# A silu in the context FFN of a two-layer diffusion backbone: formed from tanh in place of exp, add and reciprocal

## The chip, the core and the metric

One NeuronCore of a Trainium2 chip runs the whole program: TensorE (PE), VectorE (DVE), ScalarE (ACT), GpSimd (POOL), and SyncE (SP), whose queue issues most of the DMAs. The metric is the device time of one execution in microseconds (us), as the median of several runs; lower is better.

## The reference, cut to what matters

Two layers work on 1024 latent tokens of width 1024 and on 256 context tokens. Each layer has a mixer (layer 0: gated convolution beside differential attention; layer 1: pooling beside retention) and a gated ConvFFN with 2816 inner features. Context tokens go through layer 0 with the same weights, read only context tokens, and have an FFN of their own there.

```python
def conv_ffn(h, w_up, conv_w, conv_b, w_down):
    a, b = jnp.split(h @ w_up, 2, axis=-1)
    a = dwconv3(a, conv_w) + conv_b
    return (jax.nn.silu(a) * b) @ w_down
...
        x = x + g1 * y_lat
        x = x + g2 * conv_ffn(modulate(rms_norm(x, norm2_g[i]), sh2, sc2), ...)
        if not last:
            ctx = ctx + g1c * y_ctx
            ctx = ctx + g2c * conv_ffn(modulate(rms_norm(ctx, norm2_g[i]), sh2c, sc2c), ...)
```

silu(a) is a / (1 + exp(-a)), which is also a/2 times (1 + tanh(a/2)).

## The kernel before, in words

Everything is float32. A product on TensorE is made of three matmuls on split operands (`mm3`, lines 223 to 225): each operand is held as a rounded high part and the remainder, and high x high, high x low and low x high are added up. Weights stream in through SP's queue and are split on the way (`WStream.split`): line 111 rounds on ScalarE (`wh`), line 113 forms the remainder (`wl`) on VectorE, or on GpSimd for every second weight while `on_pool` is 2.

The work around the change is `attention`. Two generators are woven into each other by a fixed ratio: `att_lat`, the differential attention of the latent tokens (8 blocks of 4 query tiles; `AttBlock.scores`, `combine`, `product`), and `chain`, which takes the context tokens through output projection, norm and FFN (`ffn`, 22 feature tiles of 128). The attention's VectorE work is a maximum over the scores (tile `S`, line 1509), the combination of two softmaxes (line 1524) and the remainder of the transposed probabilities (line 1543); its exponentials are on ScalarE (line 1511).

In `ffn`, `up(f)` multiplies a tile of 128 features of both halves (tile `pab`, 48 matmuls of 256 columns), copies the halves out of PSUM on ScalarE (line 729 `a`, line 731 `b`), convolves (`conv_silu`: line 708 on ScalarE, lines 709 and 710 on VectorE, into the tile `fcv`, called `t` in the code), and forms silu(t) * b: line 736 exp(-t) on ScalarE into `e`, line 737 adds one on ScalarE, line 738 forms t * b on GpSimd, line 739 the reciprocal on VectorE, line 740 the last product on VectorE. Lines 742 and 743 split the result on ScalarE and GpSimd. After four feature tiles `down` (tile `pd`, line 757 on VectorE) multiplies them with the down weights and adds to the context. Silu itself is used as a function (line 712) only in the FFNs of the latent tokens, later in the program.

The order in which each engine gets its instructions is not written by hand: the tile framework's scheduler lays out the instructions of all engines from dependencies, program order and its own costs, and each engine then works through its queue in that order, waiting in place where an input is late. So an edit of a few instructions can change the order of others.

Of the kernel before, what the change touches and what calls it, by code (L numbers as in the profile page):

```python
# [11 lines left out]
AF = mybir.ActivationFunctionType  # L12
ALU = mybir.AluOpType
# [123 lines left out]
class Net:  # L137
# [576 lines left out]
    def ffn(self, L, xk, N, hs, G, alloc, big, ps, gate):  # L714

        nc = self.nc
        g = {}

        def up(f):
            W = self.ws.get()  # L720
            a = big.tile([P, N + 2], F32, tag="a", name="a")
            nc.gpsimd.memset(a[:, 0:1], 0.0)
            nc.gpsimd.memset(a[:, N + 1:N + 2], 0.0)

            pt = ps.tile([P, 512], F32, tag="mm", name="pab")
            self.gemm(pt[:, :N], W, hs, N, 4)
            W = self.ws.get()
            self.gemm(pt[:, N:2 * N], W, hs, N)
            nc.scalar.copy(a[:, 1:N + 1], pt[:, :N])
            b = big.tile([P, N], F32, tag="b", name="b")  # L730
            nc.scalar.copy(b, pt[:, N:2 * N])
            t = big.tile([P, N], F32, tag="cv", name="fcv")
            self.conv_silu(L, f, a, t, N, False)

            e = big.tile([P, N], F32, tag="e", name="e")
            nc.scalar.activation(e, t, AF.Exp, scale=-1.0)
            nc.scalar.activation(e, e, AF.Identity, bias=self.ones)
            nc.gpsimd.tensor_tensor(t, t, b, op=ALU.mult)
            nc.vector.reciprocal(e, e)
            nc.vector.tensor_tensor(t, t, e, op=ALU.mult)  # L740
            gt = g[f] = alloc()
            nc.scalar.copy(gt[:, 0, :], t)
            nc.gpsimd.tensor_tensor(gt[:, 1, :], t, gt.bitcast(F32)[:, 0, :], op=ALU.subtract)

        def down(f0, n):
            W = [self.ws.get() for _ in range(n)]
            for m0 in range(0, 8, 2):
                pt = ps.tile([P, 512], F32, tag="mm", name="pd")
                for m in (m0, m0 + 1):
                    po = pt[:, (m - m0) * N:(m - m0 + 1) * N]  # L750
                    ms = slice(m * P, (m + 1) * P)
                    for j in range(n):
                        gt = g[f0 + j]
                        self.mm3(po, (W[j][0][:, ms], W[j][1][:, ms]), (gt[:, 0, :], gt[:, 1, :]), j == 0, j == n - 1)
                for m in (m0, m0 + 1):
                    po = pt[:, (m - m0) * N:(m - m0 + 1) * N]
                    nc.vector.scalar_tensor_tensor(xk(m), in0=po, scalar=gate(m), in1=xk(m), op0=ALU.mult, op1=ALU.add)
                yield

        for kind, f, n in self.ffn_plan(G):  # L760
            if kind == "u":
                up(f)
                yield
            else:
                yield from down(f, n)
# [923 lines left out]
```

## Time and profile before

| what | value |
|---|---|
| median of 3 runs | 2772.87 us (2769.24 to 2776.75) |
| the profiled execution, its own time | 2781.38 us |
| its span from the first to the last instruction | 2779.6 us |
| TensorE busy | 2625.0 us, 94% |
| VectorE busy | 1910.8 us, 69% |
| ScalarE busy | 1098.5 us, 40% |
| GpSimd busy | 800.5 us, 29% |
| granted TensorE clock, mean | 0.966 of full speed |

The busy time of TensorE is the time in which at least one matmul was under way; matmuls overlap each other in the pipeline, so this share is an upper bound on how much of the engine is used. The shares are means over stages of different kinds. The stage that the change touches is the weave of attention and context FFN; its feature tiles run from about 490 to 890 us.

### The profile page before, as it was taken

Reading aid. Unit: us, or ns where it says so; the run is one execution under the profiler, and the core shown is the slowest. Engines: PE = TensorE matmul, PEld = TensorE weight load, DVE = VectorE, ACT = ScalarE, POOL = GpSimd, SP = SyncE. Lnnn points to the kernel's source line nnn. Section 1 sums busy time; section 2 is a strip of 40 time slices with the busy share of each in tenths; the row PEclk is TensorE's granted clock in tenths of the full one; section 3 lists DMA queues with packets and bytes.
Section 4 is the critical chain, followed back from the end, with each engine's and each line's share of the span. In section 5 each row is a group of like instructions: output and inputs, shape, how many; then the busy total and the mean of one; then the engine's idle time right before and its main releaser. Section 6 shows DMA issues by size and latency. Waiting matters only on the chain. (4 is left out here: it accounts for less than half of the span.)

```text
span 2779.6 us, 35344 instructions
## 1 busy us (share of the span) xinstructions
PE 2625.0 (94%) x12924; PEld 2206.8 (79%) x12924; DVE 1910.8 (69%) x2815; ACT 1098.5 (40%) x1635; POOL 800.5 (29%) x674
## 2 busy tenths in 40 slices
PE   7999998999898999999998989999999999999999
PEld 6877787888888787787886767787778888888887
DVE  7467856999887577777776665613356767766895
ACT  5322224666665344333333323323234333334342
POOL 3221113444342034444440000102212555544000
PEclk7999998999998999999999999999999999999999
DMA  6224625443322723333338774337363222224874
GB/s 246 93 93 144 197 96 164 127 131 109 109 89 79 245 84 121 114 124 121 123 105 272 246 224 153 121 112 223 115 235 114 76 84 90 85 91 152 286 231 165
DMA packets 203007, 402.26 MB, mean 145 GB/s; under 512 B 19536, under 2 KB 88784, under 8 KB 202448
## 3 DMA queue, kind: packets, MB, share of 16 engines
q1 hardware_dynamic: 199952, 394.87, 43.2%
q10 hardware_dynamic: 2880, 5.12, 0.6%
q8 instruction: 102, 1.67, 0.3%
q14 instruction: 73, 0.60, 0.1%
HBM read 330.19 MB, written 69.73 MB: 144 GB/s over the span
## 5 line engine op out<-in xcount | busy, mean ns | idle before, releaser
L225 PE MATMUL P<-s,wl 128*128 128x512 f32 x1120 | 440.4, 393 | 10.5 <-DVE wl L113 10.2
L223 PE MATMUL P<-s,wh 128*128 128x512 f32 x1120 | 438.9, 392 | 7.8 <-ACT p L884 4.5
L224 PE MATMUL P<-s,wh 128*128 128x512 f32 x1120 | 438.4, 391 | 0.0
L111 ACT CAST wh<-wr 128x1024 fp32r<-128x1024 f32 (+1 forms) x268 | 278.4, 1040 | 392.7 <-DMA wr<-in_w_dn 83.8
L113 DVE TENSOR_TENSOR wl<-wr,wh 128x1024 fp32r<-128x1024 f32 (+1 forms) x231 | 289.3, 1255 | 183.8 <-ACT wh L111 176.3
L223 PE MATMUL pd<-s,wh 128*128 128x512 f32 x660 | 263.2, 399 | 24.9 <-DVE x L938 16.3
L225 PE MATMUL pd<-s,wl 128*128 128x512 f32 x660 | 261.8, 397 | 2.5 <-DVE wl L113 2.5
L224 PE MATMUL pd<-s,wh 128*128 128x512 f32 x660 | 262.2, 397 | 0.6 <-DVE s L927 0.6
L225 PEld LDWEIGHTS P<-s,wl 128*128 128x128 f32 x1120 | 211.8, 189 | 59.2 <-DVE wl L113 15.5
L223 PEld LDWEIGHTS P<-s,wh 128*128 128x128 f32 x1120 | 212.1, 189 | 53.9 <-ACT p L884 5.4
L224 PEld LDWEIGHTS P<-s,wh 128*128 128x128 f32 x1120 | 211.9, 189 | 44.6
L363 POOL TENSOR_TENSOR rr<-vv,mhalf 128x8 f32<-128x8 f32 (+2 forms) x39 | 56.6, 1451 | 520.1 <-DVE vv L361 520.1
L223 PEld LDWEIGHTS pd<-s,wh 128*128 128x128 f32 x660 | 127.1, 193 | 54.3 <-DVE x L938 17.6
L225 PEld LDWEIGHTS pd<-s,wl 128*128 128x128 f32 x660 | 126.8, 192 | 30.7 <-DVE wl L113 4.1
L224 PEld LDWEIGHTS pd<-s,wh 128*128 128x128 f32 x660 | 127.1, 193 | 28.4 <-DVE s L927 1.5
L113 POOL TENSOR_TENSOR wl<-s,wh 128x1024 fp32r<-128x1024 f32 x40 | 101.6, 2540 | 148.0 <-ACT wh L111 148.0
L709 DVE SCALAR_TENSOR_TENSOR fcv<-a,vec,fcv 128x1024 f32<-128x1024 f32 (+1 forms) x66 | 71.1, 1078 | 102.6 <-ACT fcv L708 102.6
L111 ACT CAST wh<-r 128x1024 fp32r<-128x1024 f32 x80 | 67.1, 839 | 178.7 <-DVE r L784 99.7
L708 ACT ACTIVATE fcv<-a,vec 128x1024 f32<-128x1024 f32 (+1 forms) x66 | 68.5, 1037 | 174.5 <-POOL a L899 166.4
L113 POOL TENSOR_TENSOR wl<-wr,wh 128x1024 fp32r<-128x1024 f32 x37 | 94.3, 2550 | 134.0 <-ACT wh L111 125.5
L1511 ACT ACTIVATE p<-S,s 128x1280 f32<-128x1280 f32 (+1 forms) x80 | 92.6, 1158 | 69.5 <-DVE s L1509 65.4
L783 POOL TENSOR_TENSOR r<-r 128x512 f32<-128x512 f32 x40 | 72.5, 1813 | 132.1 <-DMA r<-in_w_up 100.9
(373 smaller groups left out, 6680.2 us busy)
## 6 DMA issues: line engine op xcount, KB each, us to landing
wr<-in_w_dn SPq DMA_DIRECT2D x101, 512.0 KB, 4.5
wr<-in_w_up SPq DMA_DIRECT2D x98, 512.0 KB, 3.6
gr<-gD SPq DMA_DIRECT2D x121, 256.0 KB, 4.0
gD<-fcv SPq DMA_DIRECT2D x44, 512.0 KB, 2.8
wr<-in_w_out SPq DMA_DIRECT2D x40, 512.0 KB, 3.7
r<-in_w_up SPq DMA_DIRECT2D x40, 512.0 KB, 3.3
s<-in_mod1T SPq DMA_DIRECT2D x136, 128.0 KB, 3.5
mbw<-in_mod0T SPq DMA_DIRECT2D x32, 512.0 KB, 3.9
```

The lines of the kernel that those rows point to most:

```text
L111: self.nc.scalar.copy(hi, raw)
L113: eng.tensor_tensor(lo, raw, hi.bitcast(F32), op=ALU.subtract)
L223: mm(out, L[0], R[0], start=first, stop=False)
L224: mm(out, L[0], R[1], start=False, stop=False)
L225: self.last_mm = mm(out, L[1], R[0], start=False, stop=last)
L363: self.last_pow = nc.gpsimd.tensor_tensor(r, vv, self.mhalf[:, :n], op=ALU.pow)
L708: nc.scalar.activation(t, a[:, 1:N + 1], AF.Identity, bias=self.v(f"fcb{L}", f), scale=w[1])
L709: nc.vector.scalar_tensor_tensor(t, in0=a[:, 0:N], scalar=w[0], in1=t, op0=ALU.mult, op1=ALU.add)
L783: nc.gpsimd.tensor_tensor(r1[:, 1536:], r1[:, 512:1024], r1[:, :512], op=ALU.add)
L1511: nc.scalar.activation(e, sv, AF.Exp, bias=s2[:, m:m + 1], accum_out=self.s1[:, qt:qt + 1] if m == 0 else s2[:, 2:3])
```

## The change

Line 731 halves `b` as it copies it; the exp becomes tanh(t/2); the ScalarE addition (line 737 before) and the reciprocal are gone, and the last product becomes one VectorE instruction that adds one to the tanh and multiplies. `t` times half of `b`, times one plus tanh(t/2), is the same product. All later lines move up by two.

```diff
             nc.scalar.copy(a[:, 1:N + 1], pt[:, :N])
             b = big.tile([P, N], F32, tag="b", name="b")
-            nc.scalar.copy(b, pt[:, N:2 * N])
+            nc.scalar.mul(b, pt[:, N:2 * N], 0.5)
             t = big.tile([P, N], F32, tag="cv", name="fcv")
             self.conv_silu(L, f, a, t, N, False)
 
             e = big.tile([P, N], F32, tag="e", name="e")
-            nc.scalar.activation(e, t, AF.Exp, scale=-1.0)
-            nc.scalar.activation(e, e, AF.Identity, bias=self.ones)
+            nc.scalar.activation(e, t, AF.Tanh, scale=0.5)
             nc.gpsimd.tensor_tensor(t, t, b, op=ALU.mult)
-            nc.vector.reciprocal(e, e)
-            nc.vector.tensor_tensor(t, t, e, op=ALU.mult)
+            nc.vector.scalar_tensor_tensor(t, in0=e, scalar=1.0, in1=t, op0=ALU.add, op1=ALU.mult)
             gt = g[f] = alloc()
```

The scheduler lays the stage out anew. Two places show how.

**VectorE, ninth feature tile.** The names: `s` and `S` belong to the attention's maximum, `xc<-pd` to the context FFN's down step, `fcv` is `t`. Before:

```order
L709 SCALAR_TENSOR_TENSOR fcv<-a,vec,fcv 128x256
L1509 TENSOR_REDUCE s_5456<-S 128x1
L710 SCALAR_TENSOR_TENSOR fcv<-a,vec,fcv 128x256
L1562 SCALAR_TENSOR_TENSOR e_5482<-ost,e_5482 128x4
L757 SCALAR_TENSOR_TENSOR xc<-pd,modB,xc 128x256 x3
L739 RECIPROCAL e<-e 128x256
L1509 TENSOR_REDUCE s_5456<-S 128x1
L740 TENSOR_TENSOR fcv<-fcv,e 128x256
```

and in the changed kernel (line 738 is the new product, 1507 the maximum, 755 the down step):

```order
L1507 TENSOR_REDUCE s_5438<-S 128x1
L709 SCALAR_TENSOR_TENSOR fcv<-a,vec,fcv 128x256
L1560 SCALAR_TENSOR_TENSOR e_5464<-ost,e_5464 128x4
L710 SCALAR_TENSOR_TENSOR fcv<-a,vec,fcv 128x256
L755 SCALAR_TENSOR_TENSOR xc<-pd,modB,xc 128x256 x2
L738 SCALAR_TENSOR_TENSOR fcv<-e,fcv 128x256
L1507 TENSOR_REDUCE s_5438<-S 128x1
```

Between the end of the convolution (line 710) and the last product stood a small instruction, three down steps, the reciprocal and a maximum; now two down steps stand there.

**ScalarE, tenth feature tile.** `p<-S` is the attention's exponential, `pth` its rounded transposed probabilities. Before:

```order
L729 COPY a<-pab 128x256
L731 COPY b<-pab 128x256
L708 ACTIVATE fcv<-a,vec 128x256
L1511 ACTIVATE p_5708,s_5689<-S,s_5689 128x1280
L736 ACTIVATE e<-fcv 128x256
L111 CAST wh<-wr 128x1024
L737 ACTIVATE e<-e,ones 128x256
L1542 CAST pth<-tpp 128x4x128 x2
```

and in the changed kernel:

```order
L729 COPY a<-pab 128x256
L731 ACTIVATE b<-pab 128x256
L708 ACTIVATE fcv<-a,vec 128x256
L111 CAST wh<-wr 128x1024 x2
L1540 CAST pth<-tpp 128x4x128 x2
L1509 ACTIVATE p_5779,s_5668<-S,s_5770 128x1280
L1540 CAST pth<-tpp 128x2x128
L736 ACTIVATE e<-fcv 128x256
L1509 ACTIVATE p_5789,s_5770<-S,s_5770 128x1280
L740 CAST s4c<-fcv 128x256
```

The tanh stands later among the attention's instructions than the exp did, the addition is gone, and no table load stands between the tanh and the exponentials on either side of it.

## Rows read from the trace of the kernel before

**Rows 1.** Busy time by stretch: us, then each engine, granted clock, DMA share, GB/s.

```profile
core 0: us, PE busy (x) PEld busy (x) DVE busy (x) ACT busy (x) POOL busy (x), PEclk, DMA share, GB/s
490.00:890.00 400.00, 362.06 (x2648) 341.62 (x2647) 356.76 (x434) 248.47 (x433) 162.66 (x137) 0.96 0.35 110
```

**Rows 2.** Instruction groups of VectorE, 490 to 890 us: count, busy us, mean ns, idle before.

```profile
L1509 DVE TENSOR_REDUCE s<-S 128x1 f32<-128x1280 f32 x59 | 87.1, 1477 | 7.2 <-PE S L1508 7.2
L739 DVE RECIPROCAL e<-e 128x256 f32<-128x256 f32 x22 | 38.4, 1746 | 1.8 <-ACT e L737 1.7
L757 DVE SCALAR_TENSOR_TENSOR xc<-pd,modB,xc 128x256 f32<-128x256 f32 x40 | 17.9, 475 | 1.2 <-PE pd L225 1.2
L710 DVE SCALAR_TENSOR_TENSOR fcv<-a,vec,fcv 128x256 f32<-128x256 f32 x22 | 17.6, 802 | 0.1
L740 DVE TENSOR_TENSOR fcv<-fcv,e 128x256 f32<-128x256 f32 x22 | 16.6, 756 | 0.2
L709 DVE SCALAR_TENSOR_TENSOR fcv<-a,vec,fcv 128x256 f32<-128x256 f32 x22 | 14.6, 665 | 8.0 <-ACT fcv L708 8.0
```

**Rows 3.** Instruction groups of TensorE in the same stretch.

```profile
L223 PE MATMUL pab<-s4c,wh 128*128 128x256 f32 x325 | 95.9, 295 | 0.0
L1507 PE MATMUL S<-k,qa 128*128 128x512 f32 x118 | 52.0, 441 | 14.0 <-ACT p L1511 13.7
L1541 PE MATMUL tpp<-ident,p 128*128 128x128 f32 x296 | 49.5, 295 | 21.7 <-DVE ptl L1543 12.8 <-DVE p L1524 7.4 <-DVE osb L1570 0.8
L379 PE MATMUL orb<-ident,r 128*128 128x128 f32 x56 | 7.7, 274 | 0.0
```

**Rows 4.** Timeline of TensorE: start, us, engine, line and operation.

```profile
655.09 0.28 PE L225 MATMUL pab<-s4c,wl 128*128 128x256 f32 x1
655.21 0.28 PE L223 MATMUL pab<-s4c,wh 128*128 128x256 f32 x1
```

**Rows 5.** Waits of ScalarE for VectorE, 490 to 890 us: total us, times, longest.

```profile
ACT p L1511 <- DVE s L1509: 39.2, 24, 4.1
```

**Rows 6.** Instruction groups of ScalarE, 490 to 890 us.

```profile
L737 ACT ACTIVATE e<-e,ones 128x256 f32<-128x256 f32 x22 | 11.2, 510 | 0.2
L736 ACT ACTIVATE e<-fcv 128x256 f32<-128x256 f32 x22 | 9.1, 415 | 10.0 <-DVE fcv L710 9.9
L731 ACT COPY b<-pab 128x256 f32<-128x256 f32 x21 | 8.0, 383 | 2.2 <-POOL fcv L738 2.2
L1552 ACT ACTIVATE osb<-pv,subg 128x256 f32<-128x256 f32 x14 | 6.6, 469 | 0.0
```

**Rows 7.** Instruction groups of GpSimd, 490 to 890 us.

```profile
L113 POOL TENSOR_TENSOR wl<-wr,wh 128x1024 fp32r<-128x1024 f32 x31 | 79.7, 2570 | 108.7 <-ACT wh L111 100.2 <-PE pd L225 8.2
L738 POOL TENSOR_TENSOR fcv<-fcv,b 128x256 f32<-128x256 f32 x22 | 22.9, 1042 | 25.3 <-ACT e L736 25.0 <-DMA wr<-in_w_up 0.3
```

**Rows 8.** Timelines of ScalarE and GpSimd at the ninth feature tile.

```profile
608.34 0.41 ACT L736 ACTIVATE e<-fcv 128x256 f32<-128x256 f32 x1
609.28 2.95 POOL L682 TENSOR_TENSOR vl<-vraw,vh 128x1280 fp32r<-128x1280 f32 x1
612.18 0.74 POOL L738 TENSOR_TENSOR fcv<-fcv,b 128x256 f32<-128x256 f32 x1
```

**Rows 9.** Timelines of VectorE, ScalarE and GpSimd at the tenth feature tile.

```profile
651.55 1.70 DVE L740 TENSOR_TENSOR fcv<-fcv,e 128x256 f32<-128x256 f32 x1
642.03 0.42 ACT L736 ACTIVATE e<-fcv 128x256 f32<-128x256 f32 x1 [2.27 <-DVE fcv L710]
642.59 1.90 POOL L738 TENSOR_TENSOR fcv<-fcv,b 128x256 f32<-128x256 f32 x1 [0.32 <-ACT e L736]
650.58 2.40 POOL L113 TENSOR_TENSOR wl<-wr,wh 128x1024 fp32r<-128x1024 f32 x1 [6.08 <-ACT wh L111]
```

**Rows 10.** One line each: durations in ns, least, median, most.

```profile
L739 DVE RECIPROCAL e<-e x22: 1736/1744/1755, 492.4 to 883.4; 128x256 f32<-128x256 f32 x22
L740 DVE TENSOR_TENSOR fcv<-fcv,e x22: 403/418/2420, 495.7 to 887.5; 128x256 f32<-128x256 f32 x22
```

## The prediction

> **What bounds the stage now.** I read the busy time by stretch first, then the groups of the busiest engine, then who waits for whom. The weave of attention and context FFN lasts some 400 us of the 2780, and in it VectorE is busy for 357 us and idle for 43 [rows 1]. TensorE shows 362 us, but that is a union of overlapping spans: a 256-column matmul is listed with 0.28 us while the next one starts 0.12 us later [rows 4]. Counting starts instead of spans: of the stage's 2648 matmuls [rows 1], 236 have 512 columns (two lines of 118) and 408 are small ones (296 transposes, and two lines of 56) [rows 3]; the other 2004 have 256 columns. Taking 0.12 us for those, twice that for 512 columns and 0.1 us for the small ones (an estimate from the spacing, at full clock) gives 240 + 57 + 41 = 338 us. So VectorE at 89% and TensorE at about 85% share the stage, ScalarE has 248 us and GpSimd 163 [rows 1]. The waits say that VectorE is more often the late one: ScalarE's exponentials stood 39.2 us for the maximum on VectorE [rows 5], TensorE's score matmuls then waited 13.7 us for these exponentials, and its transposes 12.8 and 7.4 us for VectorE directly [rows 3]. VectorE's own waits are short and spread over many releasers [rows 2]. A microsecond taken off VectorE here is therefore worth something at the end, and not a full one.
>
> **The change, part by part.** (1) The reciprocal goes: 22 times 1.746 us, 38.4 us of VectorE [rows 2]. That is nearly 11% of what it does in the stage. It is a plain saving on that queue, since nothing else in the row takes its place.
>
> (2) The last product changes from a two-input product (0.756 us mean) to an add-and-multiply of the same shape. Lines 709 and 710 are that form, with 0.665 and 0.802 us [rows 2]. Their mean, 0.734, makes 22 times -0.02, so -0.5 us, with ends of -2.0 and +1.0. I take 0.
>
> (3) ScalarE loses the addition, 22 times 0.510 = 11.2 us. The halving copy costs between nothing (0.383 us, as the copy) and 0.086 us more (0.469, the scaled copy out of PSUM of line 1552), at most 1.9 us in all [rows 6]. The tanh is taken at the exp's 0.415 us. ScalarE is idle for 152 of the 400 us, so I count nothing for its own time; if that cover were gone, it would be another 9 to 11 us. The one thing on a path is that 0.51 us leave the chain from convolution to product.
>
> (4) A wait appears. Before, the product on VectorE stood behind the reciprocal, which covered GpSimd's product t * b; line 740 waited 0.2 us in all [rows 2]. Now nothing but the scheduler's filling stands between line 710 and the new product, which needs both the tanh and, behind it, GpSimd's product (GpSimd overwrites t, which the tanh reads, so it starts after it: 642.59 behind an exp that ended at 642.45 [rows 9]). With GpSimd free, the need is 0.415 + 0.14 + 1.042 [rows 6, 7], plus a hand-over of some 0.1: 1.7 us after the convolution. What the new order puts into the gap I priced by the means of the same forms: it lies between 0 and 3.2 us, 1.8 us on average, and is below 1.7 in 12 of the 22 tiles (the ninth has two down steps there, 2 times 0.475 [rows 2]). The shortfall of these twelve adds up to 8.5 us in which VectorE stands. The ends: 0, if tanh and product run while the convolution's neighbours do, and 18 us, if GpSimd is found as late in each tile as in this trace. I take 8.5. Whatever stands behind the product in VectorE's queue waits with it: the next maximum, and so the next exponential.
>
> (5) The order of the stage is made anew, and so is that of the output projection behind it. Nothing in the rows gives a sign to this. I take 0, with 5 us on either side.
>
> So VectorE has 38.4 - 8.5 = 30 us less to go through. How much of it reaches the end? Between 0 and all. After the change VectorE needs 357 - 38 + 8.5 = 327 us, TensorE still 338: neither is slack enough to hide the other, and TensorE can go no lower. Taking about half, since the two come out level, gives **-16 us**. What is late next is TensorE's own train of matmuls, and the weight splits on ScalarE and GpSimd. Against the profiled execution that makes 2781.4 - 16 = 2765; that execution was 8.5 us above the median of the runs, so the forecast for the median is 2772.9 - 16 = **2757 us**.
>
> **A rule weighed against the rows.** A reciprocal has one input, and its 22 durations lie between 1736 and 1755 ns, whatever GpSimd was doing; the two-input product had 418 ns as its median and 2420 at most [rows 10]. At 651.55 it took 1.70 us while GpSimd's weight split ran from 650.58 to 652.98 [rows 9]. So the reciprocals are VectorE time in which GpSimd gets through its work unhindered, and that time is what goes. The Trainium skill (SBUF — State Buffer, section SBUF: two separate sides) says why the two differ: a GpSimd instruction and a VectorE instruction with two SBUF inputs take an exclusive lock on a shared port pair, and the later one fully waits. The trace agrees for the product. This gives the second rival.
>
> **The rivals.**
> - *All of it reaches the end.* If VectorE alone sets the pace, the 30 us pass through, or 38 where the new wait is covered too: 2743 to 2734 us. For it: ScalarE waits 39.2 us for the maximum [rows 5]. Against it: TensorE's 338 us. Chance 0.18.
> - *The port eats it, or TensorE paces.* GpSimd is busy for 163 of 400 us [rows 1], 41%; the reciprocals covered some 0.41 times 38.4 = 16 us of its work, which now meets two-input instructions. VectorE's net saving falls to 30 - 16 = 14 us, half of it 7: 2766 us. If TensorE's train is the pace by itself, 2773. These are one case for the chances, no difference that can be told: 0.23.
> - *The product waits for GpSimd, and VectorE's queue with it.* In the ninth tile the exp ended at 608.75, GpSimd then went into a 2.95 us split that stood first in its queue, and t * b started at 612.18, 3.4 us after it [rows 8]. If the new order put t * b behind a weight split of 2.57 us [rows 7] in every tile, the product would be ready 0.42 + 2.57 + 1.04 = 4.0 us after the convolution; less 1.8 us of filling, VectorE would stand 2.2 us in each, 22 times 2.2 = 49 us against the 38 saved: +11 us, 2784 us. It decides from 38.4 / 22 = 1.75 us of wait in a tile. Against it: GpSimd had 25.3 us of idle time before t * b, nearly all of it waiting for the exp [rows 7], so mostly it is there first. Chance 0.09.
> - *The change brings table loads.* Alternating functions could make ScalarE load a table each time. The built order shows no load in this stage, in either kernel, so nothing is put on it.
>
> **How the numbers follow.** A measurement of this kernel can tell about 0.3%, 8.3 us, from no change. The forecast's case (8 to 30 us less) has 0.50; with the first rival's 0.18 faster has 0.68. Same has 0.23, slower 0.09. The likeliest is 2757 us. The range reaches from the whole reciprocal gained (2734, less 1 for the other terms) to just above no change: 2733 to 2776. It leaves out the slower rival and a better new order.
>
> **What would show it.** In the profile of the changed kernel, VectorE's busy time in the stage should fall from 357 to about 318 us, and the stage itself from 400 to about 384. The new product should show 0.65 to 0.85 us and an idle time before it of some 5 to 12 us in total, with GpSimd's t * b as the releaser. ScalarE's wait for the maximum should shrink below 39 us. The first rival would show a stage of 370 us or less; the second, the same stage with longer two-input instructions on VectorE; the third, more than 38 us of idle time before the new product. The forecast is wrong in its mechanism if the stage shrinks though VectorE's busy share does not fall, or if the time comes from anywhere outside 490 to 930 us.

## The result, and the profile after

The changed kernel takes **2789.71 us** (median; 2779.22 to 2791.55), the kernel before 2772.87 us. The ratio is 1.0055, with a 95% interval from 1.0034 to 1.0077: slower by about 15 us, where 16 us less were forecast. One caution for what follows: the profiled execution of the change was its fastest (2779.22 us), that of the kernel before was slower than any of its timed ones (2781.38 us), so the two profiles show nearly the same span and understate the difference.

Busy time by stretch, changed kernel, the columns as in [rows 1]:

```profile
490.00:890.00 400.00, 357.60 (x2656) 335.98 (x2655) 327.31 (x413) 237.09 (x408) 154.50 (x133) 0.98 0.33 103
```

VectorE is busy for 29.5 us less than in [rows 1]. The stage itself, from the context FFN's first convolution to the last attention block, lasted 429 us before (488 to 917 us) and 434 us now (484 to 918 us): what left VectorE's work came back as idle time, and a little more.

Instruction groups of VectorE in the same stretch (the maximum is now line 1507, the down step 755, the new product 738):

```profile
L1507 DVE TENSOR_REDUCE s<-S 128x1 f32<-128x1280 f32 x59 | 87.6, 1485 | 14.5 <-PE S L1506 14.1
L709 DVE SCALAR_TENSOR_TENSOR fcv<-a,vec,fcv 128x256 f32<-128x256 f32 x21 | 23.9, 1137 | 2.5 <-ACT fcv L708 2.5
L755 DVE SCALAR_TENSOR_TENSOR xc<-pd,modB,xc 128x256 f32<-128x256 f32 x42 | 18.7, 475 | 1.3 <-PE pd L225 1.2
L710 DVE SCALAR_TENSOR_TENSOR fcv<-a,vec,fcv 128x256 f32<-128x256 f32 x21 | 17.0, 810 | 0.1
L738 DVE SCALAR_TENSOR_TENSOR fcv<-e,fcv 128x256 f32<-128x256 f32 x21 | 14.9, 710 | 10.1 <-POOL fcv L737 10.0
```

Against [rows 2]: the reciprocal and its 38.4 us are gone; the new product costs 0.710 us and stands for GpSimd for 10 us, near the forecast 8.5; the maximum waits twice as long for TensorE's scores (14.1 for 7.2). And line 709, which the change does not touch, went from 0.665 to 1.137 us. Its durations in ns (least, median, most), before and then changed:

```profile
L709 DVE SCALAR_TENSOR_TENSOR fcv<-a,vec,fcv x22: 380/482/1879, 489.1 to 875.4; 128x256 f32<-128x256 f32 x22
```

```profile
L709 DVE SCALAR_TENSOR_TENSOR fcv<-a,vec,fcv x22: 472/670/3149, 484.7 to 877.8; 128x256 f32<-128x256 f32 x22
```

Timelines of VectorE and of GpSimd in the changed kernel, ninth feature tile:

```profile
604.19 2.32 DVE L709 SCALAR_TENSOR_TENSOR fcv<-a,vec,fcv 128x256 f32<-128x256 f32 x1
...
608.71 0.42 DVE L738 SCALAR_TENSOR_TENSOR fcv<-e,fcv 128x256 f32<-128x256 f32 x1 [0.90 <-POOL fcv L737]
```

```profile
603.82 2.40 POOL L113 TENSOR_TENSOR wl<-wr,wh 128x1024 fp32r<-128x1024 f32 x1
...
607.94 0.74 POOL L737 TENSOR_TENSOR fcv<-fcv,b 128x256 f32<-128x256 f32 x1
```

This piece of the convolution starts 0.37 us behind a weight split on GpSimd and ends 0.29 us behind its end (606.51 against 606.22), for work that took 0.48 us at the median before. The rule that the prediction weighed (the Trainium skill, SBUF — State Buffer, section SBUF: two separate sides: the later of the two waits for the shared ports until the other instruction is done) says this, and the trace agrees to within some 0.2 us. Of line 709's 22 instructions 4 took over 0.9 us before, and 10 do now, each beside a split on GpSimd: the new order makes them meet GpSimd's work more often.

Waits in the same stretch, two lines of the kernel before that [rows 2] do not hold, and then those of the changed kernel (total us, times, longest):

```profile
DVE s L1520 <- ACT p L1511: 7.0, 9, 1.5
DVE ptl L1543 <- ACT pth L1542: 4.1, 7, 1.5
```

```profile
DVE s L1518 <- ACT p L1509: 15.8, 16, 3.0
DVE s L1507 <- PE S L1506: 14.1, 10, 2.4
DVE fcv L738 <- POOL fcv L737: 10.0, 13, 2.1
DVE ptl L1541 <- ACT pth L1540: 9.4, 10, 1.6
DVE osb L1568 <- PE orb L379: 6.2, 1, 6.2
PE tpp L1539 <- DVE ptl L1541: 20.8, 17, 2.3
PE S L1505 <- ACT p L1509: 8.8, 5, 4.5
ACT p L1509 <- DVE s L1507: 43.8, 32, 3.8
```

No single wait accounts for the loss; VectorE waits longer at each of the steps of the attention that are listed. ScalarE's wait for the maximum did not shrink (39.2 in [rows 5], 43.8 now), and TensorE's transposes wait 20.8 us for VectorE's remainders in place of 12.8; only its scores wait less for the exponentials, 8.8 in place of 13.7 [rows 3].

### The profile page after: what moved, and what is told of

It reads as the page before. It is cut to its first block, busy times and chain, and to the rows that moved or that the text cites. A ratio compares the mean times of both kernels' runs of the same rounds, so it can differ in the third digit from the quotient of the medians.

```text
span 2777.4 us, 35240 instructions
## 1 busy us (share of the span) xinstructions
PE 2615.2 (94%) x12924; PEld 2198.7 (79%) x12924; DVE 1882.1 (68%) x2793; ACT 1089.8 (39%) x1613; POOL 798.9 (29%) x674
## 5 line engine op out<-in xcount | busy, mean ns | idle before, releaser
L709 DVE SCALAR_TENSOR_TENSOR fcv<-a,vec,fcv 128x1024 f32<-128x1024 f32 (+1 forms) x66 | 82.1, 1244 | 99.9 <-ACT fcv L708 99.8
L1507 DVE TENSOR_REDUCE s<-S 128x1 f32<-128x1280 f32 (+1 forms) x80 | 101.8, 1272 | 17.0 <-PE S L1506 16.5
```

The costliest lines, as they stand in the source:

```text
L709: nc.vector.scalar_tensor_tensor(t, in0=a[:, 0:N], scalar=w[0], in1=t, op0=ALU.mult, op1=ALU.add)
L1507: nc.vector.tensor_reduce(s2[:, m:m + 1], sv, axis=AX.X, op=ALU.max, negate=True)
```

## Experiments

The forecast took the new order of the stage as worth nothing. To tell arithmetic and order apart, a table fixes the order in which each engine gets its instructions, by ordering dependencies without a semaphore; the arithmetic is chosen freely. The edit is the same in every kernel with a held order, only the table differs:

```diff
             n.rest(stop)
+        hold_order(tc)
...
+def hold_order(tc):
...
+    for e, packed in HELD.items():
+        seq = np.frombuffer(zlib.decompress(base64.b85decode(packed)), np.uint16)
+        for a, b in zip(seq[:-1], seq[1:]):
+            tc.add_manual_dep(ins[e][int(b)], ins[e][int(a)].name, info(), reason="held order")
```

"Old order" is that of the kernel before with the reciprocal and the addition struck out, "new order" that of the change. Ratios are to the kernel before on the same chip, with their 95% intervals; its median was 2774 to 2776 us there. A difference between two ratios is uncertain by some 5 us either way, and by 7 us where one of them is the change's.

### Arithmetic and order, apart

**e1: the change's arithmetic in the old order.** Edit: the table.

> The changed arithmetic, with every engine's instructions held in the order of the kernel before (the dropped addition and reciprocal left out; the new product stands where the old one stood). Theory ORDER (the arithmetic saves, the order that the scheduler laid anew takes it back): 10 to 30 us faster than before, 2743 to 2763. Theory WAIT (the new product's wait for GpSimd eats the saving): no faster than before, with 8 us or more of idle time before the new product, though in this order the attention's work still stands in the gap. Theory SLACK (VectorE does not set the pace of the stage): within 8 us of before, with the 38 us turned into idle time of VectorE.

Measured 2766.29 us, ratio 0.9963 [0.9950, 0.9976]: 10 us faster than before and 25 us faster than the change, with the same instructions.

**e2: the old arithmetic in the new order.** Edit: the table, on the kernel before; the reciprocal stands right ahead of the last product and the addition right behind the exp.

> The arithmetic of before, with every engine held in the order of the changed kernel (addition right behind the exp, reciprocal right ahead of the product). ORDER: slower than before by 20 to 50 us, since the bad order is there and the saving is not. SLACK: about as the changed kernel, within 8 us of 2790, since the reciprocals fit in idle time. WAIT: faster than the changed kernel, about as before, since the reciprocal again covers GpSimd's product.

Measured 2816.48 us, 1.0144 [1.0127, 1.0161]: 40 us slower with nothing but the order changed (a scheduler left free might have put the reciprocal elsewhere, so this is the price of this order).

**e3: the new order, but VectorE's step first and GpSimd's product last**, so that VectorE never stands for GpSimd there.

```diff
-            nc.gpsimd.tensor_tensor(t, t, b, op=ALU.mult)
             nc.vector.scalar_tensor_tensor(t, in0=e, scalar=1.0, in1=t, op0=ALU.add, op1=ALU.mult)
+            nc.gpsimd.tensor_tensor(t, t, b, op=ALU.mult)
```

> The changed kernel in its own order, with the two products swapped: VectorE forms t times one plus tanh first, GpSimd multiplies by half of b last, so VectorE no longer waits for GpSimd. WAIT: about 10 us faster than the changed kernel, 2780 or below, and the 11 us of idle time before the product go. ORDER and SLACK: within 6 us of the changed kernel, the idle time moves to other places.

Measured 2782.54 us, 1.0026 [1.0016, 1.0037]: 8 us below the change, give or take 7, and between the two expectations. This is a net figure. GpSimd's product kept its place in GpSimd's queue, and now GpSimd stands there for VectorE (484 to 918 us):

```profile
POOL fcv L738 <- DVE fcv L737: 39.9, 21, 3.7
```

What the wait is worth without this is taken up at e6.

**e4: before's arithmetic and order, with two more reciprocals** (44 times 1.753 = 77 us of VectorE, and the same result).

```diff
             nc.vector.reciprocal(e, e)
+            nc.vector.reciprocal(e, e)
+            nc.vector.reciprocal(e, e)
```

> The kernel before in its own order, with three reciprocals in a row for each one (the value is the same): 44 more, 77 us more of VectorE. SLACK: less than 25 us slower. ORDER, in which VectorE sets the pace while the order stays: 45 to 77 us slower, 2818 to 2850.

Measured 2845.43 us, 1.0248 [1.0232, 1.0265]: 69 us for 77, or 0.9 for each added. Some of it may be TensorE's: its granted clock in the stretch of [rows 1] was 0.91 here, 0.96 before.

The four corners: with the reciprocal the new order costs 40 us; with tanh it costs 25. In the old order the arithmetic gains 10 us, in the new one 25. Busy time of the whole stage, from the context FFN's first convolution to the last attention block: the kernel before, e2, e1, and the change.

```profile
488.00:917.00 429.00, 387.02 (x2816) 364.66 (x2814) 374.78 (x461) 261.02 (x458) 165.64 (x138) 0.95 0.34 108
```

```profile
487.00:950.00 463.00, 392.60 (x2811) 367.71 (x2810) 379.24 (x461) 262.71 (x456) 161.03 (x138) 0.94 0.32 101
```

```profile
487.00:901.00 414.00, 379.01 (x2808) 356.66 (x2807) 341.59 (x439) 250.05 (x433) 158.27 (x138) 0.97 0.35 111
```

```profile
484.00:918.00 434.00, 383.07 (x2813) 359.27 (x2811) 346.61 (x439) 251.46 (x434) 159.33 (x138) 0.97 0.34 108
```

With either arithmetic the new order makes the stage longer, by 34 us (429 to 463) and by 20 us (414 to 434), but VectorE's busy time by 4 to 5 us only (374.8 to 379.2, 341.6 to 346.6): the rest is waiting. Line 709 takes 0.677 us on average in e1, 1.132 in e2 and 1.165 in the change, all 22 counted: its slowing belongs to the order, not to the arithmetic. VectorE waits for GpSimd's product 1.0 us in e1 against 11.3 in the whole stage of the change; none of its waits grew more.

### Which part of the order

**e5: the new order with one repair.** In the changed kernel GpSimd takes the block's small power `r` behind two long splits, and TensorE and VectorE stand for it:

```profile
705.37 2.41 POOL L113 TENSOR_TENSOR wl<-wr,wh 128x1024 fp32r<-128x1024 f32 x1 [13.11 <-ACT wh L111]
707.72 2.91 POOL L682 TENSOR_TENSOR vl<-vraw,vh 128x1280 fp32r<-128x1280 f32 x1
710.58 1.02 POOL L1562 TENSOR_TENSOR r<-e,mhalf 128x4 f32<-128x4 f32 x1
```

```profile
713.84 0.69 DVE L1568 TENSOR_TENSOR osb<-osb,orb 128x512 f32<-128x512 f32 x1 [6.18 <-PE orb L379]
```

e5 puts `r` ahead of the splits, at two such places; edit: these entries of the table.

> The changed kernel in its own order, but at two places in GpSimd's queue the attention block's small power (tile r, line 1562) is put ahead of the value split (line 682) and the weight split (line 113) that it stood behind. Theory QUEUE (the part of the new order that costs is who stands behind whom in GpSimd's queue: VectorE then waits 6.2 us for the norm, and TensorE with it): 6 to 10 us faster than the changed kernel, 2780 to 2784, and the one wait of 6.2 us goes. Theory DIFFUSE (the order costs a little in many places): within 4 us of the changed kernel, 2786 to 2794.

Measured 2790.31 us, 1.0052 [1.0037, 1.0068]: no gain, though one of a few microseconds would be lost in the uncertainty. The waits of VectorE in e5:

```profile
DVE s L1507 <- PE S L1506: 16.8, 12, 3.9
DVE s L1518 <- ACT p L1509: 16.4, 16, 2.0
DVE fcv L738 <- POOL fcv L737: 14.5, 13, 4.7
DVE ptl L1541 <- ACT pth L1540: 11.7, 9, 2.5
```

The 6.2 us wait is no longer among them, and the other four, 49.3 us in the change, are now 59.4.

**s_old_then_new7, s_new_then_old7, s_only8_new, s_only5_new: the change's arithmetic in orders spliced from both**, cut at ends of attention blocks; edit: the table.

> The changed arithmetic. Every engine's order is held: that of the kernel before up to the end of the attention block that ends at 714 us in its profile, and the change's own order from there on. The two whole orders differ by 20 to 25 us with this arithmetic (2766 with the old one, 2785 to 2791 with the new one). DIFFUSE (the new order costs a little in every block): the second half costs about half of it, 2775 to 2780. PLACE (a few spots carry it; the block that ends at 777 in the change's profile lasts 63 us there against 53 with the old order): most of the cost is in this half, 2780 to 2788.

> The changed arithmetic, the reverse: the change's own order up to the same point, the old order behind it. DIFFUSE: again about half of the cost, 2775 to 2780. PLACE (the block from 714 to 777 carries it): 2766 to 2772, near the old order throughout.

> The changed arithmetic in the old order, but for one attention block, from 714 to 772 us in the profile of the kernel before, which is in the change's order. PLACE: the 10 us that this block lasts longer come out at the end, 2773 to 2778. DIFFUSE: a seventh or eighth of the whole cost, 2766 to 2770; what the block loses is then caught up behind it.

> The changed arithmetic in the old order, but for the blocks up to 614 us in the profile of the kernel before, which are in the change's order (the change reaches 616 where the old order reaches 610). PLACE at the first blocks: plus 5 to 8, 2771 to 2775. DIFFUSE: plus 5 to 8 too in the mean, but less than 3 (2765 to 2769) if the rest of the stage catches up.

| new order where | ratio | against e1 |
|---|---|---|
| nowhere (e1) | 0.9963 | |
| behind 714 us | 0.9993 [0.9984, 1.0002] | +8 us |
| up to 714 us | 1.0047 [1.0032, 1.0062] | +23 us |
| 714 to 772 us | 0.9972 [0.9961, 0.9983] | +2.5 us |
| up to 614 us | 0.9988 [0.9976, 1.0000] | +7 us |
| everywhere (the change) | 1.0055 [1.0034, 1.0077] | +25 us |

The block that lasts 10 us longer in the change's profile costs 2.5 us, at most some 7, when it alone has the new order: the suspected place does not carry the cost. The part up to 714 us costs more than either theory expected of it, the part behind it a little less than the even share. By difference (23 less 7) the two blocks between 614 and 714 us stand for some 16 us, more than any other place; no run had the new order in these two alone, so that is not shown. That 8 and 23 make 31 and not 25 lies within the uncertainty.

### Can another order be had by small edits?

**e8, e9, e10: the order left to the scheduler.** e8 is the edit of e3. e9 lets GpSimd's product go into `b`, so that it need not wait until the tanh has read `t`:

```diff
-            nc.gpsimd.tensor_tensor(t, t, b, op=ALU.mult)
-            nc.vector.scalar_tensor_tensor(t, in0=e, scalar=1.0, in1=t, op0=ALU.add, op1=ALU.mult)
+            nc.gpsimd.tensor_tensor(b, t, b, op=ALU.mult)
+            nc.vector.scalar_tensor_tensor(t, in0=e, scalar=1.0, in1=b, op0=ALU.add, op1=ALU.mult)
```

e10 does the same to the kernel before (GpSimd's product into `b`, reciprocal kept).

> The changed kernel with the two products swapped (VectorE first, GpSimd last), and the order left to the scheduler. If the wait for GpSimd is what the swap removes in any order: near the held swap, 2777 to 2788. If a newly laid order decides: anywhere from 2760 to 2800.

> The changed kernel with GpSimd's product written into b, so that it need not wait until the tanh has read t, and the order left to the scheduler. WAIT: the idle time before VectorE's product falls from 11 to below 6 us, and the time to 2780 to 2786. If a newly laid order decides: anywhere from 2760 to 2800.

> The arithmetic of before (exp, addition, reciprocal), only with GpSimd's product written into b, which gives every engine the same instructions and the scheduler another order. If a new order alone moves the time by ten microseconds and more: over 8 us from before, on either side. If not: within 5 us of 2776.

Measured 2785.95 us, 1.0034 [1.0023, 1.0045]; 2781.82 us, 1.0021 [1.0010, 1.0032]; and 2779.95 us, 1.0021 [1.0008, 1.0033]. In e9 the wait before the new product is still 9.6 us, so waiting until `t` is read is not what makes GpSimd late there. e8 and e9 lie 20 and 16 us above e1, and e10 lies 6 us above the kernel before, between its two expectations. Each order that the scheduler made anew came with a cost, from e10's 6 us up, but of e8's 20 us the swap itself may be half: it cost 10 in the old order (e6).

**e6: e3's edit in the old order**, with a second buffer for `b`.

```diff
-                big = Pool(cp, {"a": ("a", 2), "b": ("b", 1), "cv": ("cv", 2), "e": ("e", 1)})
+                big = Pool(cp, {"a": ("a", 2), "b": ("b", 2), "cv": ("cv", 2), "e": ("e", 1)})
```

> The changed arithmetic in the old order, but VectorE's add-and-multiply (on t and the tanh) comes first and GpSimd's product with the half of b last, with a second buffer for b. VectorE no longer waits for GpSimd there; in the old order that wait is only 1.0 us in all, so if GpSimd's place matters no further: 2762 to 2768. If the value that the down steps need now comes later, behind weight splits on GpSimd: 2770 or more.

Measured 2776.63 us, 0.9998 [0.9985, 1.0012]: 10 us worse than e1, where the wait was 1.0 us. GpSimd, with its product in the old place of its queue, stands for VectorE (487 to 910 us), while TensorE's down steps wait for GpSimd only 0.5 us:

```profile
POOL fcv L738 <- DVE fcv L737: 96.6, 20, 17.7
```

So the swap costs 10 us where there is no wait to remove, and in the new order it still gains 8 (e3). If it has the same cost there, the wait before the new product is worth some 18 of the order's 25 us. That is an estimate from four ratios, uncertain by 9 us, and e6 has a buffer for `b` that e3 has not; no run shows it directly.

### What the saving meets in the old order

Without the 38 us of reciprocals e1 gained 10 us, though 77 us more of them cost 69. The prediction's reason was that TensorE is level with VectorE. Four kernels, all on e1, take work from one or the other.

**f1: the attention's combining step on half of its columns** (the rest of the probabilities goes without its subtraction).

```diff
-            nc.vector.scalar_tensor_tensor(p[0], in0=p[1], scalar=s2[:, 3:4], in1=p[0], op0=ALU.mult, op1=ALU.add)
+            h = self.nk // 2
+            nc.vector.scalar_tensor_tensor(p[0][:, :h], in0=p[1][:, :h], scalar=s2[:, 3:4], in1=p[0][:, :h],
+                                           op0=ALU.mult, op1=ALU.add)
```

> The changed arithmetic in the old order (2766 us), and the attention's combining step on VectorE works on half of its columns only (the other half of the probabilities is left without its subtraction): some 30 instructions in the stage go from 1.68 us to an estimated 0.85, 25 us less on VectorE. VECTORE still paces: 0.9 of it comes out, as it did for added work, minus 22: 2744. LEVEL (VectorE and TensorE wait for each other in turn): a quarter to a half, minus 6 to minus 12: 2754 to 2760. TENSORE paces: within 4 of 2766.

Measured 2752.11 us, 0.9910 [0.9894, 0.9926], 15 us below e1. The step in e1 and then in f1, groups of VectorE in 490 to 890 us:

```profile
L1522 DVE SCALAR_TENSOR_TENSOR p<-p,s,p 128x1280 f32<-128x1280 f32 x31 | 52.2, 1683 | 0.7
```

```profile
L1523 DVE SCALAR_TENSOR_TENSOR p<-p,s,p 128x640 f32<-128x640 f32 x31 | 31.5, 1016 | 0.7
```

So 20.7 us were taken out, and 0.7 of each came out at the end (0.4 to 1 by the intervals).

**f2: one of the up step's three matmuls on 64 of 256 columns** (its correction is left out for the rest); **f3: f1 and f2 together.**

```diff
-        mm(out, L[0], R[1], start=False, stop=False)
+        c = 64 if short else out.shape[-1]
+        mm(out[:, :c], L[0], R[1][:, :c], start=False, stop=False)
```

> The changed arithmetic in the old order, and in the context FFN's up step the matmul of high by low part works on 64 of its 256 columns (that part of the correction is left out for the rest): 352 matmuls at a spacing of 0.12 us lose three quarters of it, 32 us less on TensorE. TENSORE paces: minus 22 to minus 32: 2734 to 2744. LEVEL: minus 8 to minus 16: 2750 to 2758. VECTORE paces: within 4 of 2766.

> Both of these together in the old order: 25 us less on VectorE and 32 less on TensorE. LEVEL: more than the two single gains added up, as neither then hides the other: minus 25 or more, 2741 or less. VECTORE or TENSORE: as the better of the two alone, and little more.

Measured 2771.04 us, 0.9980 [0.9968, 0.9991], and 2752.19 us, 0.9914 [0.9899, 0.9929]. They settle nothing: the group of three hardly got shorter. Timeline of TensorE in f2:

```profile
656.60 0.36 PE L226 MATMUL pab<-s4c,wl 128*128 128x256 f32 x1
656.80 0.28 PE L223 MATMUL pab<-s4c,wh 128*128 128x256 f32 x1
656.92 0.19 PE L225 MATMUL pab<-s4c,wh 128*128 128x64 f32 x1
656.95 0.36 PE L226 MATMUL pab<-s4c,wl 128*128 128x256 f32 x1
```

The matmul behind the short one is listed 0.03 us after it, but the next group then starts 0.2 us later (656.60 to 656.80). From group to group it was 0.347 us at the median, against 0.360 in e1: 0.013 us less, where 0.09 were to be taken out. In the mean it was no less, 0.375 against 0.371.

**f4: that matmul left out** (the correction is not computed), 352 matmuls fewer; **f5: f4 and f1 together.**

```diff
-        mm(out, L[0], R[1], start=False, stop=False)
+        if not up:
+            mm(out, L[0], R[1], start=False, stop=False)
```

> The changed arithmetic in the old order, and the matmul of high by low part of the context FFN's up step left out (that part of the correction is not computed): 352 matmuls fewer at 0.12 us each, 42 us less on TensorE. Ratios to the kernel before count, 0.9963 being that of the old order without this edit. TENSORE paces: at least half of the 42 us comes out, ratio 0.989 or less. LEVEL: a quarter, 10 us, ratio about 0.9925. VECTORE (the waits end with VectorE's chain of maximum, combining and remainders, and TensorE's train only fills its gaps): within 4 us, 0.995 to 0.998.

> The same, and VectorE's combining step on half of its columns (half of the probabilities is left without its subtraction), which by itself gave 0.991. LEVEL: the two gains add up or more, 0.987 or less. VECTORE: 0.990 to 0.992, as without the matmuls left out. TENSORE: as the first of these two kernels.

Measured 2761.09 us, 0.9946 [0.9930, 0.9962], and 2749.28 us, 0.9906 [0.9890, 0.9922]. From group to group it is now 0.240 us at the median. 42 us of TensorE at that spacing gave 5 us at the most likely, with an uncertainty that takes in nothing, and with f1's edit they gave no more than f1 alone, within 6 us. TensorE's waits in e1, then in f4, 490 to 890 us:

```profile
PE S L1505 <- ACT p L1509: 12.9, 8, 3.1
PE tpp L1539 <- DVE ptl L1541: 10.2, 10, 2.5
PE tpp L1539 <- DVE p L1522: 6.8, 4, 2.2
```

```profile
PE S L1506 <- ACT p L1510: 20.4, 16, 3.1
PE tpp L1540 <- DVE ptl L1542: 18.8, 14, 3.2
PE tpp L1540 <- DVE p L1523: 10.5, 8, 3.0
```

The three grew from 29.9 to 49.7 us: TensorE's free time became waiting for the attention's exponentials and for VectorE. Busy time by stretch in e1, then in f4:

```profile
490.00:890.00 400.00, 367.61 (x2730) 346.28 (x2730) 333.91 (x428) 246.07 (x423) 155.44 (x134) 0.97 0.35 109
```

```profile
490.00:890.00 400.00, 344.20 (x2414) 318.53 (x2413) 335.58 (x435) 247.57 (x427) 157.44 (x136) 0.94 0.34 109
```

TensorE is busy for 344 us in place of e1's 368. Its granted clock is 0.94 in place of 0.97, and in the mean a group still takes 0.266 us in place of 0.371, so that some 37 of the 42 us were taken out after all. TensorE's own work does not pace this stage in the old order.

## Why the prediction was wrong

**The step that failed is (5):** "Nothing in the rows gives a sign to this. I take 0, with 5 us on either side." The new order costs 25 us with the new arithmetic (e1 against the change) and 40 with the old (e2). That alone turns the sign. Term (4) did hold one piece of the order, 8.5 us of standing, of which half was to reach the end. So of the some 30 us between forecast and result 21 are the order beyond (4), and 9 the share that reaches the end: half of 38 us would have been 19 in an order without that wait, and e1 gave 10. The range held only the orders near the old one, and the text itself left "a better new order" out while it forgot a worse one.

**How much reaches the end** was the right sort of question with the wrong reason. The prediction took half of 30 us "since the two come out level", TensorE's train being late next. In the old order 10 us came out (e1), a third of the 33 us by which VectorE's busy time in the stage fell (374.8 to 341.6), but f4 and f5 show that TensorE's work was no cover. What became of the rest shows in VectorE's waits in e1, 490 to 890 us:

```profile
DVE s L1507 <- PE S L1506: 17.0, 19, 3.3
DVE ptl L1541 <- ACT pth L1540: 10.0, 12, 1.6
```

The maximum now waits 17.0 us for the scores (7.2 in [rows 2]) and the remainders 10.0 us for ScalarE's rounding, 4.1 before. In f4, with less work for TensorE, the maximum waits no less, 19.6 us. A microsecond inside the attention's own chain, as f1's, was worth 0.7; a reciprocal, which stands beside that chain, about 0.3 when taken out and 0.9 when added. That the chain through maximum, exponential, combining, transposes and remainders sets the pace fits all of these runs; f1 took VectorE's work and a link of that chain at once, and no run shortened the chain and left VectorE's work as it was, so it is a reading and not shown.

**(1) and the port.** Of the 38.4 us, VectorE's busy time in the stage lost 28.2 (374.8 to 346.6): some 10 us went into slower two-input instructions, line 709 alone 11.0 (14.6 to 25.6 us in the whole stage). The second rival named this (16 us by its sum), as a consequence of the missing reciprocals. e1 and e2 show that the order did it: in e1, without reciprocals, the line takes 14.9 us, in e2, with them, 24.9.

**(2) and (3)** held: 0.697 us for the product, 0.418 for the tanh, 0.394 for the halving copy, and no table loads.

**(4)** held in what it said of VectorE: 8.5 us forecast, 11.3 measured, in 14 tiles with 2.1 us at most. At the end the wait may have cost more than the half that was forecast: 8 us net by e3, give or take 7, and perhaps twice that (e6).

**The rivals.** The first would have needed a stage shorter by 30 us; it got 5 us longer. The third forecast slower, but by 38 us and more of waiting for GpSimd; there were 11.3. Slower came with far less of that wait, by an order whose cost no rival named.

**What stays open.** Which property of the new order costs the time. The two places that stood out do not carry it (e5, s_only8_new). The wait before the new product is the best candidate, with 8 to 18 of the 25 us, and by difference the two blocks from 614 to 714 us; neither was tested alone. Of the 25 us, 20 show as a longer stage in the profiled executions of e1 and the change (414 to 434 us).

## What to carry to other kernels

Where a scheduler lays out the queues, an edit is two changes: the work that it takes out, and the order made anew. Hold the old order and run the new arithmetic in it, before you judge either; here the arithmetic was worth 10 us in the old order and the new order cost 25. e1, 2766.29 us, is the version that beats both kernels.

A busy share near 90% does not make an engine the pace: take work from that engine alone (f4, f1) and see what comes out.

## What the hardware showed that was not expected

- A matmul cut from 256 to 64 columns saved 0.013 us in a group of three with 128 x 128 weights (0.360 to 0.347 us at the median); left out as a whole it saved 0.120 (0.240 in f4).
- A 128 x 256 add-and-multiply on VectorE that met a GpSimd split took up to 3.15 us in place of 0.48, and the mean of its line rose by 0.5 us through order alone (0.677 us in e1, 1.165 in the change).
